# HGRN heads as a pipeline of levels and states, with the first pair's queries and forget gates made by seven products and kept in DRAM

## The chip, the cores and the metric

The kernel runs on one core of one Trainium2 chip. A core has TensorE (PE in the profile, its weight loads PEld), VectorE (DVE), ScalarE (ACT), GpSimd (POOL) and SyncE (SP), which issues most of the DMA. The metric is the device time of one execution in microseconds, as the median of several runs. Every engine works through its own row of instructions in the order in which the program puts them; a scheduler in the building layer sets that order, so it is not the order of the Python lines.

## The reference

One layer of a decoder trunk over 1024 tokens of width 1024, all in float32. A combined projection `u @ w_in` gives ten groups of columns, and two branches mix the tokens. What the change touches is the first branch, HGRN2, with 8 heads of 128:

```python
q = silu(q)                                   # per head (S, 128)
f = lb + (1 - lb) * sigmoid(zf);  k = (1 - lb) * sigmoid(-zf)
S_t = diag(f_t) S_{t-1} + k_t^T v_t           # state 128 x 128
o_t = S_t^T q_t                               # then head norm and output gate
```

The second branch is retention with 4 heads. Both are projected (`w_pa`, `w_pb`), merged by gates, projected again (`w_o`) and normed; then comes an MLP with a squared ReLU.

## The kernel before

Each float32 product is made of three products of rounded parts (`mm3`, lines 182 to 186: high by high, high by low, low by high), 128x128 weights against 512 columns. A plain tile of 128 output columns takes 8 blocks of rows, so 24 such products for each half of the tokens (`dense_T`, line 383). Where four blocks are needed together, `seven` (line 437) makes 2x2 blocks with seven products instead of eight: 84 large products for a group of 256 columns instead of 96. A `use_...` function then takes each of the group's four result blocks.

The program runs in stages.

- A start stage makes the scaled input and four gate tiles.
- A first stage by sevens makes the row-wise groups `hi`, `rv`, `rg` (`seven_rows`) and then 16 kept groups (`hg`, `ga`, `rq`, `rk`; list `kept`, lines 1563 to 1574), whose results go to DRAM by DMAs that GpSimd issues.
- A second stage has plain products. `r_head(0)`, the first retention head, is woven with the last eight halves of the gate `gb` (`gate_proj`). Then come the HGRN heads.
- After them the first part of retention's merge (`r_first`: 16 pieces of 12 products with `w_pb`), the other retention heads with the HGRN merge (`r_fill`), the output projection and the MLP.

An HGRN head has two parts, both in `h_rec` (line 796). In the levels the scores of 128 tokens are built from 2 tokens upward: VectorE scales q and k by products of forget gates (lines 804 to 868), TensorE multiplies k by the scaled q (lines 811 and 847, into two PSUM banks of the kind `a`), and VectorE copies the wanted entries into the score tile with masks (lines 814, 815, 862). In the states TensorE transposes k (line 878) and then, for each of eight chunks, adds state and score parts of the output (889, 890) and makes the update (895), which VectorE adds to the state (898, 900). Norm, transposes (920) and the gate (924) follow some steps later through a list of deferred calls (`later`, `tick`).

`h_rec` gives way 9 times in the levels and 10 times in the states, and one head follows the other. Between its steps `h_fill` puts halves of the plain projections `hq` and `hf` (`h_cols`, line 765): four halves of 24 products a head. Six halves of the first pair go ahead of all, then 26 are woven with 123 steps; the last 31 steps are mixed with 14 pieces of `r_first` and five steps of retention head 1. The scaled q of a head lives in one large tile `hX` from its first level to its last chunk.

Large tiles come from 14 buffers (`U`), the gates f and k from 4 buffers (`fk`). Retention head 0 uses the same `fk` buffers and six of the `U` buffers for its own states.

Of the kernel before, what the change touches and what calls it, by code (L numbers as in the profile page):

```python
# [19 lines left out]
P = 128  # L20
# [3 lines left out]
HH = 8  # L24
# [29 lines left out]
PB_END, R1_N, R1_AT = 36, 5, 20  # L54
# [3 lines left out]
H_DEFER = (6, 8)  # L58
# [72 lines left out]
class Trunk:  # L131
# [590 lines left out]

    def use_turned(self, dst):
# [29 lines left out]
    def h_dense(self, p):  # L753
        self.hst[p] = [dict(), dict()]
        self.h_values(p)
        for hd in (0, 1):
            for what in ("hq", "hf"):
                yield from self.h_cols(p, what, hd)

    def h_fill(self, begun):  # L760
        yield from begun
        for p in range(1, 4):
            yield from self.h_dense(p)
# [26 lines left out]
    def h_values(self, p):  # L790
        v = self.hv[p % 2]
        self.hst[p][0]["v"] = self.hst[p][1]["v"] = v
# [3 lines left out]
    def h_rec(self, p, hd):  # L796
# [3 lines left out]
        q, f, k, v = s["q"], s["f"], s["k"], s["v"]  # L800
# [27 lines left out]
        for ln, sz in enumerate(H_SIZES):  # L828
# [5 lines left out]
            D4 = self.xp.tile([P, B], F32, tag=f"D{2 * ln + 2}", bufs=1, name=self.uid("D"))  # L834
# [32 lines left out]
            V.tensor_tensor(Xv[:, 0, 1], Xv[:, 0, 1], by(Dv[:, 0], B, sz), op=ALU.mult)  # L867
            V.tensor_tensor(Xv[:, 0, 2:4], Xv[:, :, 2], by(D2v[:, 0], 2, B, sz), op=ALU.mult)
            Dt = D4
        yield  # L870
        state = None
        for hf in (0, 1):
# [7 lines left out]
            nc.scalar.activation(kt, pb, AF.Copy)  # L880
            ob, sq = (self.e2().rearrange("p (c e) -> p c e", c=4) for _ in (0, 1))
            ms = self.xp.tile([P, 4], F32, tag="ms", bufs=2, name=self.uid("ms"))
            for c in range(4):
                n = 4 * hf + c
                cs = slice(n * P, n * P + P)
                vn = v[:, n, hd * P:(hd + 1) * P]
                po = self.ps("c", (P, P))
                if n > 0:
                    nc.tensor.matmul(po, qp[:, cs], state, start=True, stop=False)
# [3 lines left out]
                if n < 7:  # L893
# [7 lines left out]
                    state = ns  # L901
                yield
            nc.vector.tensor_scalar(ms, ms, 1.0 / P, HEAD_EPS, op0=ALU.mult, op1=ALU.add)
            rs = self.xp.tile([P, 4], F32, tag="rs", bufs=2, name=self.uid("rs"))
            nc.gpsimd.tensor_tensor(rs, ms, self.mhalf[:, :4], op=ALU.pow)
            self.later(2, lambda ob=ob, rs=rs, hf=hf, g=g: self.h_scale(p, h, hf, ob, rs, g))
            yield

    def h_scale(self, p, h, hf, ob, rs, g):
# [4 lines left out]
        self.later(H_DEFER[p // 3] - 2, lambda: self.h_out(h, hf, ob, g))  # L914
# [12 lines left out]
    def h_pair_rec(self, p, heads=(0, 1)):  # L927
        for hd in heads:
            for _ in self.h_rec(p, hd):
                self.tick()  # L930
                yield
        while heads[-1] == 1 and p == 3 and self.pend:
            self.tick()
            yield

# [603 lines left out]
def build(ctx, tc, ins, out):  # L1539
# [11 lines left out]
    k.or_d = dt("or_d", RH, 512)  # L1551
    k.rq_d, k.rk_d = dt("rq_d", RH, 256), dt("rk_d", RH, 256)
# [16 lines left out]
    for h in range(RH):  # L1569
# [3 lines left out]
        kept.append((("rk", h), C_RK + 256 * h, k.use_turned(k.rk_d[h])))  # L1573
    kept += light
# [3 lines left out]
    for p in range(4):  # L1578
# [67 lines left out]
    with ExitStack() as s:  # L1646
# [3 lines left out]
        weave(k.gate_proj("gb", k.gb_d, range(4, KT)), k.r_head(0), 8, 12)  # L1650
# [9 lines left out]
        begun = k.h_dense(0)  # L1660
        for _ in range(6):
            k.tick()
            next(begun)
        rec = (x for p in range(4) for x in k.h_pair_rec(p))
        weave(k.h_fill(begun), islice(rec, 123), 26, 123)
        pb, r1 = k.r_first(), k.r_head(1)
        for _ in range(2):
            next(pb)
        mix((rec, 31, 0, 31), (pb, 14, 0, PB_END), (r1, R1_N, R1_AT, 36))
# [81 lines left out]
```

## Time and profile before

| what | value |
|---|---|
| median of the runs shown | 2287.32 us (2284.84 to 2288.99) |
| the profiled execution's own time | 2287.82 us |
| its span, first to last instruction | 2286.0 us |
| mean granted clock of TensorE | 0.997 |
| kept groups by sevens | about 490 to 766 us |
| retention head 0 with gates | about 766 to 868 us |
| first product of an HGRN head (line 804) | 879.4 us for the first head, 1151.2 us for the eighth |

A stretch is named by its times from the span's start. In a row of busy time by stretch each engine has its busy microseconds and, in brackets, its instructions; then come the granted clock, the busy share of the DMA engines and what they moved in GB/s. In a row of the groups by line stand busy time and mean ns of one instruction, and behind the next bar the engine's idle time just before them. A row of the waits names who waited, for whom, the sum, how often, and the longest. TensorE's float32 matmuls leave two records each, its transposes and rounded products one. Matmuls overlap, so two that follow each other at full speed start closer together than their listed length.

### The profile page before, as it was taken

How to read it: one execution, taken by the hardware profiler on the slowest of the kernel's cores; microseconds unless marked ns; L12 is line 12 of the kernel's file. 1: busy time of each engine (PE TensorE's matmuls, PEld its weight loads, DVE VectorE, ACT ScalarE, POOL GpSimd, SP SyncE). 2: the span in 40 equal slices, each digit the busy share in tenths (PEclk: the TensorE clock that was granted, in tenths of full speed). 3: DMA queues.
4: the chain of work that ended last, by engine and by line, in shares of the span. 5: the costliest groups of instructions: out<-in, count | busy, mean ns of one | idle time of the engine just before them, and what ended most of it. 6: DMA issues, size and time to landing. Idle time of an engine off the chain costs nothing.

```text
span 2286.0 us, 29888 instructions
## 1 busy us (share of the span) xinstructions
PE 2239.7 (98%) x10366; PEld 1847.6 (81%) x10366; DVE 1642.2 (72%) x3054; ACT 1013.8 (44%) x1861; POOL 290.8 (13%) x458
## 2 busy tenths in 40 slices
PE   7999999999999999999999999999999999999998
PEld 5888888888888788888877788888878888888886
DVE  8966768686778465788866667767896666668778
ACT  4433434453333362333446556222475555643441
POOL 0111011111111020010011222013112111100001
PEclk9999999999999999999999999999999999999999
DMA  9766655533333542121225666864244444877863
GB/s 277 239 216 230 228 187 198 173 120 111 111 111 102 176 152 83 42 88 56 88 92 178 232 197 213 298 211 164 84 159 173 152 152 152 280 263 239 260 219 116
DMA packets 227320, 389.85 MB, mean 171 GB/s; under 512 B 17480, under 2 KB 122688, under 8 KB 226400
## 3 DMA queue, kind: packets, MB, share of 16 engines
q1 hardware_dynamic: 197376, 291.20, 39.5%
q0 software_dynamic: 29616, 96.67, 11.4%
q8 instruction: 82, 1.34, 0.2%
q14 instruction: 70, 0.57, 0.1%
q10 hardware_dynamic: 176, 0.06, 0.0%
HBM read 286.14 MB, written 101.72 MB: 170 GB/s over the span
## 4 chain that ended last, share of the span: by engine, by line
PE 69%; issue 17%; DVE 5%; DMA 4%; POOL 3%; ACT 2%; SPq 0%; POOLq 0%; DVEq 0%; ACTq 0%
PE psd L185 13%; PE psd L186 13%; PE psd L184 13%; PE psa L185 3%; PE psa L184 3%; PE psa L186 3%; PE psc L185 3%; PE psc L184 3%; PE psc L186 3%; PE psb L1130 2%; PE psa L847 2%; PE psb L185 1%; PE psb L186 1%; PE psb L184 1%; PE psc L1116 1%
## 5 line engine op out<-in xcount | busy, mean ns | idle before, releaser
L184 PE MATMUL psd<-U,wh 128*128 128x512 f32 x760 | 305.7, 404 | 3.5 <-ACT e L1224 2.2
L185 PE MATMUL psd<-U,wh 128*128 128x512 f32 x760 | 303.4, 399 | 2.8 <-DVE U L180 2.8
L186 PE MATMUL psd<-U,wl 128*128 128x512 f32 x760 | 302.0, 398 | 0.0
L179 ACT ACTIVATE bh<-s 128x512 fp32r<-128x512 f32 x204 | 128.0, 633 | 247.6 <-PE psd L185 62.0
L184 PE MATMUL psd<-U,bh 128*128 128x512 f32 x496 | 193.0, 389 | 1.8 <-DVE e L446 1.8
L179 ACT ACTIVATE bh<-raw 128x512 fp32r<-128x512 f32 x153 | 97.2, 637 | 217.2 <-PE psd L185 85.8
L185 PE MATMUL psd<-U,bh 128*128 128x512 f32 x496 | 193.1, 389 | 0.1
L186 PE MATMUL psd<-U,bl 128*128 128x512 f32 x496 | 193.0, 389 | 0.0
L180 DVE TENSOR_TENSOR bl<-raw,bh 128x512 fp32r<-128x512 f32 x153 | 104.5, 689 | 113.0 <-ACT bh L179 112.6
L180 DVE TENSOR_TENSOR bl<-s,bh 128x512 fp32r<-128x512 f32 x204 | 139.2, 687 | 61.6 <-ACT bh L179 61.4
L184 PEld LDWEIGHTS psd<-U,wh 128*128 128x128 f32 x760 | 142.9, 189 | 32.6 <-ACT U L179 3.6
L185 PEld LDWEIGHTS psd<-U,wh 128*128 128x128 f32 x760 | 143.9, 189 | 30.9 <-DVE U L180 5.1
L186 PEld LDWEIGHTS psd<-U,wl 128*128 128x128 f32 x760 | 143.7, 189 | 27.5
L179 ACT ACTIVATE wh<-raw 128x512 fp32r<-128x512 f32 (+1 forms) x87 | 61.3, 729 | 207.0 <-PE psd L185 187.7
L179 ACT ACTIVATE U<-hr 128x512 fp32r<-128x512 f32 x112 | 70.4, 630 | 145.8 <-issue 80.2
L180 DVE TENSOR_TENSOR U<-hr,U 128x512 fp32r<-128x512 f32 x112 | 77.0, 687 | 51.4 <-ACT U L179 51.3
L184 PEld LDWEIGHTS psd<-U,bh 128*128 128x128 f32 x496 | 93.1, 188 | 21.7 <-DVE e L446 2.6
L185 PEld LDWEIGHTS psd<-U,bh 128*128 128x128 f32 x496 | 93.1, 188 | 19.8 <-DVE U L180 0.5
L186 PEld LDWEIGHTS psd<-U,bl 128*128 128x128 f32 x496 | 93.1, 188 | 19.4
L184 PE MATMUL psa<-U,bh 128*128 128x512 f32 x248 | 96.7, 390 | 1.9 <-ACT e L434 1.9
L180 DVE TENSOR_TENSOR wl<-raw,wh 128x512 fp32r<-128x512 f32 (+1 forms) x87 | 69.9, 817 | 37.6 <-ACT wh L179 35.1
L185 PE MATMUL psa<-U,bh 128*128 128x512 f32 x248 | 96.5, 389 | 0.0
(431 smaller groups left out, 5577.8 us busy)
## 6 DMA issues: line engine op xcount, KB each, us to landing
raw<-in_w_in SPq DMA_DIRECT2D x146, 512.0 KB
raw<-in_w_down SPq DMA_DIRECT2D x64, 512.0 KB
raw<-in_w_ada SPq DMA_DIRECT2D x32, 512.0 KB
raw<-in_w_up SPq DMA_DIRECT2D x32, 512.0 KB
raw<-in_w_pb SPq DMA_DIRECT2D x20, 512.0 KB
adw<-in_w_ada SPq DMA_DIRECT2D x16, 512.0 KB
v_d<-e POOLq DMA_DIRECT2D x32, 256.0 KB, 4.3
rg_d<-e POOLq DMA_DIRECT2D x32, 256.0 KB, 2.6
```

The source lines that it names most:

```text
L179: self.nc.scalar.activation(hi, src, AF.Copy)
L180: self.nc.vector.tensor_tensor(lo, src, hi.bitcast(F32), op=ALU.subtract)
L184: r = mm(out, wh, uh, start=start, stop=False, skip_group_check=more)
L185: mm(out, wh, ul, start=False, stop=False, skip_group_check=more)
L186: return r, mm(out, wl, uh, start=False, stop=stop, skip_group_check=more)
L847: nc.tensor.matmul(pa[:, c * 192:(c + 1) * 192].rearrange("p (b w r) -> p b w r", w=2, r=3 * sz), k[:, n * P:(n + 1) * P], mv, start=True, ...
L1116: mm(G[e], l[:, n % 2, es], r, start=n == 0 and i == 0, stop=i == 2, skip_group_check=n > 0)
L1130: mm(po, l, r, start=i == 0, stop=i == len(pairs) - 1)
```

## The change

It does three things.

- The groups `hq` and `hf` of the first pair of heads become two more kept groups of the first stage. `use_query` and `use_forget` make q, f and the sigmoid for k there, and GpSimd's DMAs store them to `q_d`, `f_d`, `k_d`. In the second stage `h_load` brings them back, and `h_fill` covers only pairs 1 to 3.
- `h_rec` is split into `h_levels` and `h_states`. `h_stream` takes one step of the states of head h-1 and one of the levels of head h in turn, nine of each, so that 81 steps hold all heads. The last level writes the scaled q into two small tiles `Q` (with two copies on ScalarE), so that `hX` is free for the next head, and the last scan factors get two buffers.
- The weaving has new numbers. One half of the gate `gb` comes ahead of retention head 0, five are woven with it, two come behind. Of the 81 steps, 4 to 63 are mixed with 24 halves, from 63 on with the 16 pieces of `r_first`, and from 72 on with three steps of retention head 1.

```diff
+H_SEVEN = (0,)
+GB_N, H_LOAD = 5, 5
+H_FILL = 63
+PB_END, R1_N, R1_AT = 85, 3, 72
-H_DEFER = (6, 8)
+H_DEFER = ((1, 2), (2, 3))
+H_STEPS = 9
...
+    def use_query(self, p):
+        def use(m, half, src, bank):
+            ...
+            nc.scalar.activation(sg, src, AF.Sigmoid)
+            nc.vector.scalar_tensor_tensor(tv, pr, self.omlb[:, h:h + 1], sr, op0=ALU.mult, op1=ALU.mult)
+            nc.gpsimd.dma_start(self.q_d[h].rearrange("p (w b) -> p w b", w=2)[:, :, half * 256:half * 256 + 256], tv)
+    def use_forget(self, p):
+        def use(m, half, src, bank):
+            ...
+            nc.scalar.activation(f, src, AF.Sigmoid)
+            nc.scalar.activation(t, src, AF.Sigmoid, scale=-1.0)
+            nc.scalar.activation(f, f, AF.Identity, scale=self.omlb[:, h:h + 1], bias=self.lb[:, h:h + 1])
+            nc.gpsimd.dma_start(self.f_d[h][:, sl], f)
+            nc.gpsimd.dma_start(self.k_d[h][:, sl], t)
...
+    def h_load(self, p, hd):
+        s["q"], s["f"], s["k"] = self.hq[hd], self.e4(), self.e4()
+        nc.sync.dma_start(s["q"][:, 0:2], self.q_d[h].rearrange("p (w b) -> p w b", w=2))
+        nc.sync.dma_start(s["f"], self.f_d[h])
+        nc.sync.dma_start(s["k"], self.k_d[h])
...
+            if last:
+                Q = s["Q"] = [self.e2() for _ in (0, 1)]
+                for hf in (0, 1):
+                    nc.scalar.activation(Qv[:, 0], Xv[:, 0, 0, bs], AF.Copy)
+                    V.tensor_tensor(Qv[:, 1], Xv[:, 0, 1, bs], by(Dv[:, 0, bs], B // 2, sz), op=ALU.mult)
+                    V.tensor_tensor(Qv[:, 2:4], Xv[:, :, 2, bs], D2v[:, 0, bs].unsqueeze(1).to_broadcast([P, 2, B // 2]).unsqueeze(3).to_broadcast([P, 2, B // 2, sz]), op=ALU.mult)
...
-                    nc.tensor.matmul(po, qp[:, cs], state, start=True, stop=False)
+                    nc.tensor.matmul(po, Q[hf][:, c * P:(c + 1) * P], state, start=True, stop=False)
...
+    def h_stream(self):
+        states = iter(())
+        for h in range(HH + 1):
+            p, hd = divmod(h, 2)
+            levels = self.h_levels(p, hd) if h < HH else iter(())
+            if hd == 1 and p < 3:
+                self.h_values(p + 1)
+            for n in range(H_STEPS):
+                next(states, None)
+                next(levels, None)
+                ...
+                self.tick()
+                yield
+            if h < HH:
+                states = self.h_states(p, hd)
...
+    for p in H_SEVEN:
+        kept += [(("hq", p), C_HQ + 256 * p, k.use_query(p)), (("hf", p), C_HF + 256 * p, k.use_forget(p))]
...
-        weave(k.gate_proj("gb", k.gb_d, range(4, KT)), k.r_head(0), 8, 12)
+        gates = k.gate_proj("gb", k.gb_d, range(4, KT))
+        drain(islice(gates, 1))
+        weave(islice(gates, GB_N), k.r_head(0), GB_N, 12)
...
-        begun = k.h_dense(0)
-        for _ in range(6):
-            k.tick()
-            next(begun)
-        weave(k.h_fill(begun), islice(rec, 123), 26, 123)
-        mix((rec, 31, 0, 31), (pb, 14, 0, PB_END), (r1, R1_N, R1_AT, 36))
+        for hd in (0, 1):
+            k.h_load(0, hd)
+            if hd == 0:
+                k.h_values(0)
+        rec, pb, r1 = k.h_stream(), k.r_first(), k.r_head(1)
+        mix((gates, 6 - GB_N, 0, 4), (rec, 4, 0, 4))
+        nf, n = 8 * (4 - len(H_SEVEN)), 9 * H_STEPS
+        mix((rec, n - 4, 4, n), (k.h_fill(), nf, 4, H_FILL), (pb, 16, H_FILL, PB_END), (r1, R1_N, R1_AT, n))
```

What this does to the engines' rows is seen at three places. Line numbers of the changed kernel are 4 higher up to `h_cols`, some 40 higher in the levels (804 became 844, 811 became 851, 847 became 888) and 58 to 78 higher behind (878 became 936, 889 to 895 became 953 to 959, 920 became 986, 1103 became 1181).

On SyncE, before, at the end of retention head 0: its last loads of `rg_d` and `v_d`, the values of the first pair (`hi_d`), and then weights.

```order
L1103 DMA e_7449<-rg_d_93 128x512
L1084 DMA e_7452<-v_d_89 128x512
L794 DMA U_7558<-hi_d_97 128x8x256
L1103 DMA e_7522<-rg_d_93 128x512
L336 DMA raw_7169<-in_w_in 128x4x256
```

On SyncE now, at the same place: the loads of q, f and k of both heads of the pair stand there.

```order
L1162 DMA e_7768<-v_d_89 128x512
L800 DMA hq_7844<-q_d_103 128x1024
L801 DMA fk_7848<-f_d_111 128x1024
L1181 DMA e_7810<-rg_d_93 128x512
L802 DMA fk_7849<-k_d_119 128x1024
L834 DMA U_7846<-hi_d_97 128x8x256
L800 DMA hq_7845<-q_d_104 128x1024
L801 DMA fk_7854<-f_d_112 128x1024
L802 DMA fk_7855<-k_d_120 128x1024
```

The six loads are in front of the weights, and the last load of retention head 0 (`rg_d`) stands between them. On VectorE, before, where retention head 0 ends: its last norm (lines 1154 to 1157), then the q of the dense halves (786), weight splits (180), and only then the first head's product of q and f (804).

```order
L1154 BN_AGGR stat_7535<-stat_7535 128x2
L1155 TENSOR_SCALAR stat_7535<-stat_7535 128x1
L1157 SCALAR_TENSOR_TENSOR U_7066<-U_7066,stat_7535,e_7522 128x512
L786 SCALAR_TENSOR_TENSOR hq_7556<-psd_7575,small,e_7600 128x2x256
L180 TENSOR_TENSOR wl_7640<-raw_7165,wh_7639 128x512
L786 SCALAR_TENSOR_TENSOR hq_7556<-psd_7611,small,e_7636 128x2x256
L180 TENSOR_TENSOR wl_7640<-raw_7167,wh_7639 128x512
L180 TENSOR_TENSOR wl_7712<-raw_7169,wh_7711 128x512
L804 TENSOR_TENSOR hq_7556<-hq_7556,fk_7645 128x512
```

On VectorE now, at the same place (844 is the product of q and f, 1231 to 1235 retention head 0's last norm, 865, 880 and 881 the scan factors):

```order
L844 TENSOR_TENSOR hq_7844<-hq_7844,fk_7848 128x512
L865 TENSOR_TENSOR hq_7844<-fk_7848 128x512
L1231 BN_STATS stat_7823<-U_7416 128x6
L880 TENSOR_TENSOR D_7961<-hq_7844 128x2x128
L1232 BN_AGGR stat_7823<-stat_7823 128x2
L881 TENSOR_TENSOR D_7962<-D_7961 128x128
L1233 TENSOR_SCALAR stat_7823<-stat_7823 128x1
L1235 SCALAR_TENSOR_TENSOR U_7416<-U_7416,stat_7823,e_7810 128x512
```

The product that needs the loaded q and f has moved ahead of retention head 0's last norm. On TensorE, before, in the first head's states (psc): transposes of k (878), then chunk by chunk the products 889, 890 and 895, with large products (184 to 186) between.

```order
L895 MATMUL psc_7979<-U_7558,e_7970 128x128
L878 MATMUL psb_8050<-cst,fk_7646 128x128 x4
L186 MATMUL psd_8143<-U_272,wl_7774 128x512
L184 MATMUL psd_8143<-U_272,wh_7773 128x512
L889 MATMUL psc_8018<-st_7981,U_7555 128x128
L890 MATMUL psc_8018<-U_7558,U_7550 128x128
L895 MATMUL psc_8023<-U_7558,e_7970 128x128
```

On TensorE now, in the states of the fourth head: the first bank products (851) of the next head's levels stand between the chunks (953, 954, 959).

```order
L954 MATMUL psc_9291<-U_7847,U_7838 128x128
L959 MATMUL psc_9295<-U_7847,e_9257 128x128
L851 MATMUL psa_9299<-hq_7844,fk_8965 128x3x64 x2
L851 MATMUL psa_9304<-hq_7844,fk_8965 128x3x64 x2
L986 MATMUL psb_9309<-cst,e_9090 128x128 x4
L953 MATMUL psc_9317<-st_9297,e_9238 128x128
L954 MATMUL psc_9317<-U_7847,U_7838 128x128
L959 MATMUL psc_9322<-U_7847,e_9257 128x128
L188 MATMUL psd_9383<-U_296,wh_8958 128x512
L189 MATMUL psd_9383<-U_297,wh_8958 128x512
L851 MATMUL psa_9326<-hq_7844,fk_8965 128x3x64 x2
```

Levels of one head and states of the one before it share TensorE's row. All large products together are 8412 in the row before and 8388 now.

More of the change, by code (lines that the diff above doesn't have):

```diff
@@ L721, in use_gate @@
         return use
+    def use_query(self, p):
+        def use(m, half, src, bank):
+            nc = self.nc
+            h = 2 * p + m
+            sg, t = self.et(), self.et()
+            nc.scalar.activation(sg, src, AF.Sigmoid)
+            pr, sr = (a.rearrange("p (b two) -> p two b", two=2) for a in (src, sg))
+            tv = t.rearrange("p (two b) -> p two b", two=2)
+            nc.vector.scalar_tensor_tensor(tv, pr, self.omlb[:, h:h + 1], sr, op0=ALU.mult, op1=ALU.mult)
+            nc.gpsimd.dma_start(self.q_d[h].rearrange("p (w b) -> p w b", w=2)[:, :, half * 256:half * 256 + 256], tv)
+        return use
+    def use_forget(self, p):
+        def use(m, half, src, bank):
+            nc = self.nc
+            h = 2 * p + m
+            sl = slice(half * 512, half * 512 + 512)
+            f, t = self.et(), self.et()
+            nc.scalar.activation(f, src, AF.Sigmoid)
[3 more added lines that the diff above has]
+            nc.gpsimd.dma_start(self.k_d[h][:, sl], t)
+        return use
     def use_turned(self, dst):
@@ L758, in h_dense, with h_fill @@
                 yield from self.h_cols(p, what, hd)
[L760 to L763, printed above, removed]
+    def h_fill(self):
+        for p in range(4):
+            if p not in H_SEVEN:
+                yield from self.h_dense(p)
+    def h_load(self, p, hd):
+        nc = self.nc
+        h = 2 * p + hd
+        s = self.hst.setdefault(p, [dict(), dict()])[hd]
+        s["q"], s["f"], s["k"] = self.hq[hd], self.e4(), self.e4()
+        nc.sync.dma_start(s["q"][:, 0:2], self.q_d[h].rearrange("p (w b) -> p w b", w=2))
+        nc.sync.dma_start(s["f"], self.f_d[h])
+        nc.sync.dma_start(s["k"], self.k_d[h])
     def h_cols(self, p, what, hd):
@@ L880, in h_rec @@
             nc.scalar.activation(kt, pb, AF.Copy)
+            return g, kt
+        state = None
+        nxt = turned(0)
+        yield
+        for hf in (0, 1):
+            g, kt = nxt
             ob, sq = (self.e2().rearrange("p (c e) -> p c e", c=4) for _ in (0, 1))
@@ L925, in h_out @@
         nc.gpsimd.dma_start(self.oh_d[h][:, hf * 512:hf * 512 + 512], ot)
-    def h_pair_rec(self, p, heads=(0, 1)):
-        for hd in heads:
-            for _ in self.h_rec(p, hd):
+    def h_stream(self):
[8 more added lines that the diff above has]
+                next(levels, None)
+                if n == H_LOAD and h > 0 and (h + 1) // 2 in H_SEVEN:
+                    self.h_load((h + 1) // 2, (h + 1) % 2)
                 self.tick()
                 yield
-        while heads[-1] == 1 and p == 3 and self.pend:
+            assert next(levels, None) is None
+            if h < HH:
+                states = self.h_states(p, hd)
+        while self.pend:
             self.tick()
@@ L1577, in build @@
     plain = [k.spec_T(w_in, 0, C_GB + 256 * m, ("gb", m), ("U" if m == 2 else "w", "w")) for m in (2, 3)]
-    for p in range(4):
+    for p in (p for p in range(4) if p not in H_SEVEN):
         plain.append(k.in_turn(*(k.spec_T(w_in, 0, c0 + 256 * p, (c, p)) for c, c0 in (("hq", C_HQ), ("hf", C_HF)))))
```

53 lines of the change are left out of this document (30 added, 23 removed).

## The prediction

> **What bounds the kernel now.** I read the page's busy times first, then busy time by stretch of the span, then the waits inside those stretches.
>
> ```profile
> span 2286.0 us, 29888 instructions
> PE 2239.7 (98%) x10366; PEld 1847.6 (81%) x10366; DVE 1642.2 (72%) x3054; ACT 1013.8 (44%) x1861; POOL 290.8 (13%) x458
> ...
> PE 69%; issue 17%; DVE 5%; DMA 4%; POOL 3%; ACT 2%; SPq 0%; POOLq 0%; DVEq 0%; ACTq 0%
> ```
>
> TensorE is busy 98% of the span, and the chain that ended last is its own work. Matmuls overlap, so busy time hides small losses; the price of a product is its spacing. The stretches below are: sixteen groups by seven products; retention head 0 with gate products; the first dense halves and the first HGRN head; four whole HGRN heads; the last two heads; the join to the last retention heads; these heads; and ten microseconds inside the last-two-heads stretch.
>
> ```profile
> core 0: us, PE busy (x) PEld busy (x) DVE busy (x) ACT busy (x) POOL busy (x), PEclk, DMA share, GB/s
> 490.00:766.00 276.00, 275.72 (x1217) 228.07 (x1216) 198.45 (x319) 104.70 (x175) 31.34 (x59) 1.00 0.34 113
> 766.00:868.00 102.00, 99.72 (x475) 81.22 (x474) 48.58 (x85) 50.28 (x86) 19.82 (x31) 1.00 0.48 160
> 868.00:949.80 81.80, 81.15 (x409) 68.24 (x408) 54.48 (x137) 26.43 (x66) 3.15 (x4) 1.00 0.22 71
> 949.80:1113.50 163.70, 161.84 (x883) 137.67 (x881) 132.90 (x357) 59.99 (x183) 12.83 (x16) 1.00 0.19 63
> 1113.50:1235.00 121.50, 114.76 (x620) 96.11 (x619) 83.74 (x207) 55.57 (x172) 15.47 (x23) 0.99 0.31 107
> 1235.00:1290.00 55.00, 51.15 (x237) 39.31 (x236) 42.60 (x71) 38.03 (x61) 14.18 (x21) 1.00 0.75 255
> 1223.00:1233.00 10.00, 10.00 (x62) 8.93 (x61) 4.41 (x10) 5.99 (x21) 1.17 (x3) 0.83 0.27 93
> ```
>
> The first row gives the price: 276.00 us for 1217 products of 512 columns, 0.227 us each, with nothing lost. TensorE's visible idle time lies elsewhere: 2.3 us with retention head 0, 6.7 us in the last two HGRN heads (121.50 less 114.76), 3.9 us at the join. In the last two heads the granted clock also falls to 0.83 over ten microseconds, worth 1.7 us more. Four heads in the middle take 163.70 us, 40.9 each, and VectorE is busy 132.90 of them: 33.2 a head, 81%. So TensorE bounds every stage, with VectorE closest behind it in the HGRN heads.
>
> What a head costs TensorE comes from these rows of the groups by line and of the chain; the times at the chain's front are for so many matmuls in a row.
>
> ```profile
> L847 PE MATMUL psa<-U,fk 128*128 128x192 f32 x384 | 73.4, 330 | 1.7 <-DVE U L862 0.7 <-ACT U L855 0.4 <-DVE U L837 0.4
> L811 PE MATMUL psa<-hq,fk 128*128 128x192 f32 x128 | 26.5, 329 | 0.2 <-ACT U L855 0.2
> L889 PE MATMUL psc<-st,U 128*128 128x128 f32 x112 | 24.9, 304 | 4.1 <-ACT e L891 2.6 <-ACT e L892 0.8 <-DVE st L900 0.4
> L890 PE MATMUL psc<-U,U 128*128 128x128 f32 x128 | 24.7, 275 | 0.0
> L895 PE MATMUL psc<-U,e 128*128 128x128 f32 x112 | 22.5, 283 | 1.6 <-ACT e L891 0.8 <-ACT e L880 0.7
> L920 PE MATMUL psb<-cst,e 128*128 128x128 f32 x64 | 9.7, 273 | 0.0
> L878 PE MATMUL psb<-cst,fk 128*128 128x128 f32 x64 | 9.6, 273 | 0.0
> ...
> 916.18 1.30 PE psa L847 x8
> 1301.11 1.78 PE psa L1064 x16
> ```
>
> Levels: 64 records a head at 1.30/8 = 0.1625 us, 10.4 us. States: 60 records a head at 1.78/16 = 0.111 us, 6.7 us. Together 17.1 us. The four dense halves a head (24 products each) are 21.8 us. Sum 38.9, measured 40.9: 2.0 us a head are lost to small waits and to changing between small and large matmuls.
>
> **The change, part by part.** All of it is set against the profiled execution: 2287.8 us, of which the span is 2286.0; the median of the shown runs, 2287.3, lies 0.5 us lower.
>
> *Products.* The four column tiles of pair 0 took 8 halves of 24 products; by sevens, two groups take 7 blocks of 12 each: 168 instead of 192. 24 x 0.227 = **-5.4 us**, with bounds close by, since both stages run at that spacing. The 12 stores that it adds go through GpSimd's queue, 13% busy. In the stage that takes the two groups, VectorE is busy 198.45 of 276.00 and ScalarE 104.70: the added sigmoids and products find room there, and TensorE idles 0.28 us in it now. I cost them at nothing; were ScalarE to hold up a weight split, it would be one or two split lengths, a microsecond.
>
> *Start of retention head 0.*
>
> ```profile
> PE psa L1050 <- DMA e<-rq_d: 1.8, 1, 1.8
> ...
> 782.10 6.41 DMA e<-v_d
> 788.57 5.67 DMA e<-rq_d
> ```
>
> TensorE waits 1.8 us for the retention loads. Now a whole gate half is issued ahead, and the order puts eight more large products (1.8 us) before the first transposes that need them: **-1.8 us** (bounds -1.8 and 0).
>
> *Rest of retention head 0.* Five gate halves are woven in instead of eight; three have gone ahead of it or behind it. From about its fourth block on, the blocks follow each other with hardly a large product between.
>
> ```profile
> 817.49 2.06 PE psb L1130 x9
> ...
> 821.59 2.05 PE psb L1130 x9
> ```
>
> Two such blocks stand 4.10 us apart now; their 15 products and four transposes are 3.85 us. So about 0.25 us is lost per bare block, 1 us over four: **+1 us** (0 to 2).
>
> *Start of the HGRN heads.* Before, six dense halves (32.7 us) stood between retention head 0 and the first bank of levels. Now the head's q, f and k come from DRAM and about 15 us of TensorE work (50 large products, 11.4; 17 transposes, 1.9; two banks, 1.3) lie between the retention product that frees the buffers of f and k and the second pair of banks. VectorE must in that time get the loads, make q*f and its scan factors, finish retention's last norm and copy two banks. Its rows:
>
> ```profile
> L814 DVE COPY_PREDICATED U<-mask,psa 128x256 f32<-128x256 uint8 x32 | 14.1, 452 | 7.1 <-PE psa L811 7.0
> L815 DVE COPY_PREDICATED U<-mask,psa 128x128 f32<-128x128 uint8 x32 | 14.0, 443 | 0.4
> L820 DVE TENSOR_TENSOR U<-hq,fk 128x1024 f32<-128x1024 f32 x8 | 9.8, 1224 | 1.3 <-PE psc L889 1.3
> L837 DVE TENSOR_TENSOR U<-U,hq 128x512 f32<-128x512 f32 x8 | 5.5, 693 | 0.2
> ```
>
> Four copies (1.8), L820's product (1.2), four of the 512-wide kind (2.8) and the small ones, some 3, make 9 us behind a landing; with the 5.67 us of the 256 KB load in the chain above that is 14.7, about even with the cover. The second head's q and f, for which VectorE stops a little later in its row, stand behind 3.4 MB of loads. At the 255 GB/s of the join they land after 13 us, at the 160 GB/s of retention head 0 after 21. I take **+2.5 us**, nearer to the fast row, since nothing else loads there; bounds 0 and +8 (21 less 15, and the copies behind). The Trainium skill (DMA: Bandwidth & Descriptors, Anatomy of one DMA) fits a transfer, measured on the GpSimd path, as 2.0 us plus bytes over 436 GB/s. By that estimate the loads land after 9.8 us and this term would be 0, the sum 2.5 us lower; the 256 KB loads above (5.67 us in the chain) are slower than its 2.6.
>
> *The heads in the middle.* While dense halves last, 59 steps (6.6 heads) carry 24 of them: 3.66 a head, 20.0 us, and 17.1 of its own: 37.1. With today's loss of 2.0 a head it would be 39.1; the shorter head is work already counted, not gain. But the margin of VectorE shrinks (33.2 of 39.1 is 85%), and in its row state updates of one head now stand between copies of the next.
>
> ```profile
> DVE U L862 <- PE psa L847: 11.2, 16, 1.1
> DVE st L900 <- PE psc L895: 7.2, 10, 1.1
> DVE st L898 <- PE psc L895: 3.8, 4, 1.0
> DVE U L814 <- PE psa L811: 3.0, 10, 0.3
> ```
>
> These are its waits for TensorE in the four-head stretch: 25.2 us, 6.3 a head. 33.2 + 6.3 = 39.5: its own loop is as long as TensorE's. Where two loops are that even, each adds some of the other's waits: I take 0.5 us a head, **+3.3 us**; bounds 0, and +11.9 (the head stays at 40.9, 1.8 more than 39.1).
>
> *The last two heads.* Their 6.7 us of idle time and the 1.7 us of clock come from one head's states standing alone, with too few products of w_pb between (14 pieces over the end). The longest single wait there is short:
>
> ```profile
> PE psd L184 <- ACT e L1224: 1.7, 1, 1.7
> PE psc L889 <- ACT e L891: 1.4, 2, 0.7
> ```
>
> The Trainium skill (TensorE: Matmul & The Clock Gate, Part 1) has the clock halve after an idle window of about 3.4 us. Here it halved for that long (0.83 over 10 us) with no listed wait over 1.7, so the row decides: many short waits are enough. By that rule a start of the heads at its bound of 8 us idle would halve the clock too and cost 1.7 us more, 2288.6 in all.
>
> Now head 6's states lie under head 7's levels, 16 w_pb pieces of 2.7 us begin when the dense halves end, and only head 7's nine state steps are bare, each with a piece beside it. I leave 2.4 of the 8.4 us: **-6 us** (bounds -8.4 and -2). The join stays as it was, since the last output must still go to DRAM and back.
>
> Sum: -5.4 - 1.8 + 1 + 2.5 + 3.3 - 6 = -6.4; 2287.8 - 6.4 = 2281.4, and about 2281 against the median.
>
> **The rivals.** *VectorE becomes the bound (slower).* If every one of a head's seven state updates makes VectorE wait as L900 does now (7.2/10 = 0.72 us), that is 5.0 instead of 1.8 a head, its loop is 42.7, and 6.6 x (42.7 - 39.6) = 20 us come on top: 2302. For it: 85%, and a queue with two heads' work in one row. Against it: the order puts levels between the products on which a state update waits. It decides from 40.6 us a head on; there the gain of 6.4 is gone. Chance 0.13.
>
> *Late loads (no change).* The loads land at the slow rate, VectorE stands at q*f with retention's last norm behind it, and TensorE waits the 8 us of the upper bound: 2287. For it: no dense half is left as cover. Against it: the queue has little else. Chance 0.11.
>
> *The waits only move (no change).* The last heads keep their idle time, for instance because head 7's states now meet all that was put at the end: -0.4 us, 2287. Chance 0.13.
>
> *More than forecast.* The start costs nothing, the middle nothing more than today, the end its whole 8.4 and half of the 3.9 us at the join: -5.4 - 1.8 - 8.4 - 2 = -17.6, 2270. For it: the pipeline gives TensorE two independent heads to take work from. Against it: VectorE's 85%. Chance 0.11.
>
> **How the numbers follow.** The forecast has the other 0.52; its own range is 2275 to 2287. The range from 2270 to 2291 takes in all but the VectorE rival and the outermost starts. 0.2% is 4.6 us, about what a measurement of this kernel tells from no change. Faster: 0.9 of the forecast and the large gain, 0.58. Same: the rest of the forecast, the moved waits and most of the late loads, 0.27. Slower: the VectorE rival, and the worst of the late loads, 0.15.
>
> **What would show it.** In the profile after: 24 fewer large products; no wait of TensorE for rq_d; starts of successive heads 39 to 40.5 us apart while dense halves last (over 40.6: VectorE rival, with its busy share near 85% and longer waits for L959); a wait of 1 to 4 us of TensorE for VectorE at the first head (8: late loads); under 3 us idle in the last two heads and no dip of the clock. If the product count falls by 24 and the time doesn't fall, the middle terms were mis-sized.

## The result, and the profile after

| | before | after |
|---|---|---|
| median | 2288.15 us (2284.84 to 2289.6, 4 runs) | 2265.87 us (2264.62 to 2269.01, 4 runs) |
| ratio, 95% interval | | 0.9907 (0.989 to 0.9924) |
| profiled span | 2286.0 us | 2264.0 us |
| a second set, timed with the last experiments | 2287.99 us | 2270.38 us, 0.992 (0.9906 to 0.9933) |

The change saves 18 to 22 us where 6.4 were forecast. The direction was right. The first median lies outside the stated range of 2270 to 2291, the second at its edge. These lines of the page of the changed kernel answer to the first ones of before: span, busy times and instructions, and the engines' shares of the chain that ended last.

```profile
span 2264.0 us, 29935 instructions
PE 2224.8 (98%) x10342; PEld 1847.5 (82%) x10342; DVE 1649.2 (73%) x3090; ACT 1026.4 (45%) x1889; POOL 299.6 (13%) x470
...
PE 91%; DVE 2%; DMA 2%; issue 2%; ACT 1%; POOL 1%; SPq 0%; DVEq 0%; ACTq 0%; POOLq 0%
```

TensorE has 24 matmuls fewer (10366 before), and still 98% of the span. Busy time by stretch, in the order of the stretches shown of before: groups by seven products; retention head 0 and the start of the heads; five heads in the middle; the last two heads in two pieces; what follows them.

```profile
core 0: us, PE busy (x) PEld busy (x) DVE busy (x) ACT busy (x) POOL busy (x), PEclk, DMA share, GB/s
528.00:804.00 276.00, 276.00 (x1220) 228.52 (x1219) 195.11 (x308) 105.17 (x179) 34.27 (x63) 1.00 0.34 116
804.00:900.00 96.00, 93.91 (x450) 76.07 (x449) 55.53 (x104) 49.50 (x85) 21.07 (x32) 1.00 0.59 204
930.60:1117.60 187.00, 186.87 (x1053) 165.52 (x1051) 157.25 (x448) 75.13 (x233) 17.87 (x20) 1.00 0.19 65
1105.00:1181.00 76.00, 75.05 (x424) 65.79 (x423) 65.20 (x171) 39.53 (x124) 10.75 (x15) 1.00 0.34 116
1181.00:1223.00 42.00, 38.69 (x217) 32.47 (x216) 18.33 (x31) 26.90 (x72) 8.73 (x14) 1.00 0.47 164
1223.00:1275.00 52.00, 51.64 (x236) 41.93 (x236) 38.41 (x68) 32.25 (x51) 11.58 (x17) 0.97 0.79 262
```

The stage by seven products runs at the price of before (276.00 over 1220 products). The third row is the surprise: five heads (930.6 and 1117.6 are starts of line 863, the same place in two heads) take 187.0 us, 37.4 each, where the forecast said 39.6. TensorE is busy 186.87 of 187.00, and VectorE, 84% busy, holds nothing up. TensorE's waits at the start of the heads (the first line), and then in the last two heads:

```profile
PE psa L1243 <- ACT U L1236: 1.6, 2, 1.4
...
PE psb L986 <- ACT e L977: 3.3, 1, 3.3
PE psa L888 <- ACT U L896: 0.6, 1, 0.6
```

No wait for `rq_d` is left. One long wait stands at the very end, where the last head's output is scaled (977) before it is turned (986).

**Lost time.** Small losses don't show in busy time, so I took from each trace, for every matmul, the time until the next one starts, less the median of that time for the same shape in the same trace. The sum over the medians is called work, the sum of the differences lost time. The stretches are: to the first transposes of retention head 0; to the first bank of levels; 240 us from there on, some six heads; from there to the last head's last output; all that follows.

| us | work | to retention 0 | to first bank | heads, 240 us | heads, rest | after | lost in all |
|---|---|---|---|---|---|---|---|
| before | 2209.4 | 22.5 | 1.2 | 10.9 | 14.6 | 15.3 | 64.5 |
| after | 2203.6 | 22.1 | 3.9 | 4.7 | 7.5 | 9.9 | 48.2 |
| after, second execution | 2203.4 | 21.0 | 4.0 | 4.6 | 7.3 | 17.1 | 54.0 |

Work fell by 5.8 us. Lost time fell by 16.3 in one execution and by 10.5 in another; in both, the heads give 13 of it, and the stretch after them is what differs.

### The profile page after: what moved, and what is told of

Same layout as the page of the kernel before. It is cut to its first block, busy times and chain, and to the rows that moved or that the text cites. A ratio compares the mean times of both kernels' runs of the same rounds, so it can differ in the third digit from the quotient of the medians.

```text
span 2264.0 us, 29935 instructions
## 1 busy us (share of the span) xinstructions
PE 2224.8 (98%) x10342; PEld 1847.5 (82%) x10342; DVE 1649.2 (73%) x3090; ACT 1026.4 (45%) x1889; POOL 299.6 (13%) x470
## 3 DMA queue, kind: packets, MB, share of 16 engines
q0 software_dynamic: 30576, 99.82, 11.9%
## 4 chain that ended last, share of the span: by engine, by line
PE 91%; DVE 2%; DMA 2%; issue 2%; ACT 1%; POOL 1%; SPq 0%; DVEq 0%; ACTq 0%; POOLq 0%
PE psd L189 17%; PE psd L190 17%; PE psd L188 17%; PE psa L189 5%; PE psa L188 5%; PE psa L190 5%; PE psc L189 3%; PE psc L188 3%; PE psc L190 3%; PE psa L888 2%; PE psb L1208 2%; PE psb L190 1%; PE psb L189 1%; PE psb L188 1%; PE psc L1194 1%
## 5 line engine op out<-in xcount | busy, mean ns | idle before, releaser
L188 PE MATMUL psd<-U,wh 128*128 128x512 f32 x696 | 279.6, 404 | 0.0
L189 PE MATMUL psd<-U,wh 128*128 128x512 f32 x696 | 277.0, 398 | 1.8 <-DVE U L184 1.8
L190 PE MATMUL psd<-U,wl 128*128 128x512 f32 x696 | 276.6, 398 | 0.0
L188 PE MATMUL psd<-U,bh 128*128 128x512 f32 x528 | 205.5, 389 | 1.3 <-DVE e L450 1.3
L189 PE MATMUL psd<-U,bh 128*128 128x512 f32 x528 | 205.5, 389 | 0.0
L190 PE MATMUL psd<-U,bl 128*128 128x512 f32 x528 | 205.4, 389 | 0.0
L189 PEld LDWEIGHTS psd<-U,wh 128*128 128x128 f32 x696 | 131.5, 189 | 27.0 <-DVE U L184 3.4
L190 PEld LDWEIGHTS psd<-U,wl 128*128 128x128 f32 x696 | 131.4, 189 | 25.4
L188 PEld LDWEIGHTS psd<-U,wh 128*128 128x128 f32 x696 | 130.8, 189 | 24.6 <-ACT U L183 1.0
L188 PEld LDWEIGHTS psd<-U,bh 128*128 128x128 f32 x528 | 99.1, 188 | 22.5 <-DVE e L450 2.1
L189 PEld LDWEIGHTS psd<-U,bh 128*128 128x128 f32 x528 | 99.1, 188 | 21.2 <-DVE U L184 0.5
L190 PEld LDWEIGHTS psd<-U,bl 128*128 128x128 f32 x528 | 99.1, 188 | 20.5
L188 PE MATMUL psa<-U,bh 128*128 128x512 f32 x264 | 102.9, 390 | 0.4 <-ACT e L438 0.3
L189 PE MATMUL psa<-U,bh 128*128 128x512 f32 x264 | 102.7, 389 | 0.0
L190 PE MATMUL psa<-U,bl 128*128 128x512 f32 x264 | 102.7, 389 | 0.0
```

Source lines behind the costliest of these rows:

```text
L188: r = mm(out, wh, uh, start=start, stop=False, skip_group_check=more)
L189: mm(out, wh, ul, start=False, stop=False, skip_group_check=more)
L190: return r, mm(out, wl, uh, start=False, stop=stop, skip_group_check=more)
```

## The experiments

The theory after the result: what came beyond the products comes from the pipeline, because a state step that stands alone makes TensorE wait, and under another head's levels it doesn't. The rivals: it comes from pair 0's way (no dense halves before the first head, gate halves moved, less work on ScalarE and VectorE), or from the last two heads alone. Beside that stood the question why VectorE had not become the bound. Diffs are against the changed kernel. The lost time of all of them but 5 and 6 is in one table behind the first four.

**1. The pipeline alone** (label pipe_only): pair 0 by dense halves again, in the places of before.

```
-H_SEVEN = (0,)
+H_SEVEN = ()
...
+        weave(k.gate_proj("gb", k.gb_d, range(4, KT)), k.r_head(0), 8, 12)
...
+        begun = k.h_dense(0)
+        for _ in range(6):
+            k.tick()
+            next(begun)
...
+        mix((rec, n, 0, n), (k.h_fill(begun), 26, 0, H_FILL), (pb, 16, H_FILL, PB_END), (r1, R1_N, R1_AT, n))
```

> The pipeline over heads alone: pair 0's queries and forget gates are dense halves again, six of them ahead of the first head as in the kernel before, all eight gate halves are woven with retention head 0, and nothing goes through DRAM for them. Theory (the pipeline saves what came beyond the products): the 5.4 us of products and the 1.8 us of the rq_d wait are not gained, nearly all of the rest is, so 2271 to 2275 us; in the profile the loss of TensorE in the heads falls as in the changed kernel (from about 19 us to about 8). Rival (the gain beyond the products comes from pair 0's way: no dense halves before the first head, three gate halves moved, less work on VectorE and ScalarE per head): 2284 to 2290. By the prediction's own terms for the middle and the last heads (+3.3 and -6) it would be 2285.

Measured: 2274.83 us, ratio 0.9941 (0.9928 to 0.9953): 15 us of the change's 18 to 22. The theory had it. The lost time in the heads is halved, 12.7 us against 25.5 in the table below, where the expectation named about 8 and 19.

**2. Pair 0 by seven products alone** (label seven_only): levels and then states of one head, twice nine steps.

```
-H_DEFER = ((1, 2), (2, 3))
+H_DEFER = ((2, 4), (2, 6))
...
+            for part in (self.h_levels(p, hd), self.h_states(p, hd)):
+                for n in range(H_STEPS):
+                    next(part, None)
+                    self.tick()
+                    yield
...
+        nf, n = 8 * (4 - len(H_SEVEN)), 16 * H_STEPS
+        mix((rec, n - 4, 4, n), (k.h_fill(), nf, 4, 116), (pb, 16, 116, 150), (r1, R1_N, 128, n))
```

> Pair 0 by seven products and through DRAM alone, with the gate halves where the change puts them: the states of a head follow its own levels again, a step at a time, and the dense halves and w_pb pieces are spread over the steps in the proportion of the kernel before. The copy of the scaled queries at the last level stays. Theory (pipeline): only products, the rq_d wait and a start that costs some 2 us are left, so -5.4 - 1.8 + 2 = -5, 2283 us; the heads in the middle stay about 2 us above their work. Rival (pair 0's way): 2266 to 2272.

Measured: 2280.17 us, 0.9966 (0.9952 to 0.9979), 9 us faster than before against 5 expected, and 10 to 14 us slower than with the pipeline. The two parts alone make 24 us, the whole 18 to 22: they add up, near enough.

**3. The overlap at the last two heads alone** (label last_two).

```
-H_DEFER = ((1, 2), (2, 3))
+H_DEFER = ((2, 4), (2, 3))
...
+            if h < 7:
+                for _ in range(H_STEPS if h > 0 else 0):
+                    next(states, None)
+                    self.tick()
+                    yield
             for n in range(H_STEPS):
                 next(states, None)
                 next(levels, None)
...
+        nf, n = 8 * (4 - len(H_SEVEN)), 15 * H_STEPS
+        mix((rec, n - 4, 4, n), (k.h_fill(), nf, 4, 117), (pb, 16, 117, 139), (r1, R1_N, 126, n))
```

> The changed kernel with the states of heads 0 to 5 after the head's own levels, as in the kernel before, and only head 6's states under head 7's levels; dense halves and w_pb pieces in the same proportion to the heads. It splits the pipeline's gain between the middle and the last two heads. The prediction's terms say that the overlap costs 3.3 us in the middle and saves 6 at the end: this kernel would then be faster than the changed one, 2262 to 2265. Theory now (the overlap saves in the middle too, about 1 us a head, since the loss of 2.0 us a head came from the states standing alone): the serial sevens kernel had 2280, the end gives back 5 to 7 of it, so 2273 to 2275, some 8 above the changed kernel. Rival (all of the gain lies in the last two heads): 2266.

Measured: 2282.6 us, 0.9976 (0.9967 to 0.9986). A miss: the overlap at the end alone gains nothing against the serial order. The prediction's terms would have made this the fastest of all.

**4. The overlap everywhere but there** (label first_six): head 6's states alone, then head 7's levels.

```
+            if h == 7:
+                for _ in range(H_STEPS):
+                    next(states, None)
+                    self.tick()
+                    yield
...
+        nf, n = 8 * (4 - len(H_SEVEN)), 10 * H_STEPS
+        mix((rec, n - 4, 4, n), (k.h_fill(), nf, 4, 66), (pb, 16, 66, 92), (r1, R1_N, 81, n))
```

> The complement of the run with the overlap at the last two heads alone: here heads 0 to 6 are pipelined, and head 6's states stand alone before head 7's levels. With the overlap at the end alone nothing was gained against the serial order (2282.6 against 2280.2, each against the kernel before: 0.9976 and 0.9966). If the gain is the middle's (about 0.6 us a head less lost by TensorE, since no product waits for a state alone, 7 us in all), this kernel keeps 7 of the 14 us or more: 2271 to 2274. If the overlap pays only as a whole, because each waits for the other, it stays near 2280.

Measured: 2267.9 us, 0.9913 (0.9899 to 0.9927): as fast as the changed kernel, and 3 us faster than the theory named. The overlap of heads 0 to 6 carries the pipeline's whole gain, as far as the spread between executions lets it be told.

The same 187 us of the span, 930 to 1117, in six traces; all of it lies in the heads. TensorE's busy time is the first number behind the length, VectorE's the third. Before, then seven_only, then last_two:

```profile
930.00:1117.00 187.00, 184.49 (x1003) 157.01 (x1002) 151.86 (x404) 69.58 (x212) 15.02 (x20) 1.00 0.19 63
```

```profile
930.00:1117.00 187.00, 182.47 (x1005) 157.28 (x1004) 153.12 (x428) 70.35 (x218) 15.86 (x20) 1.00 0.19 64
```

```profile
930.00:1117.00 187.00, 182.98 (x1003) 156.16 (x1002) 151.17 (x419) 70.56 (x221) 16.25 (x20) 1.00 0.19 64
```

The pipelined ones, pipe_only, first_six and the changed kernel's second execution:

```profile
930.00:1117.00 187.00, 186.82 (x1052) 165.36 (x1052) 159.08 (x451) 75.96 (x237) 16.52 (x19) 1.00 0.19 64
```

```profile
930.00:1117.00 187.00, 186.77 (x1059) 165.27 (x1058) 161.28 (x458) 75.50 (x236) 18.00 (x21) 1.00 0.20 65
```

```profile
930.00:1117.00 187.00, 186.89 (x1051) 165.50 (x1050) 157.33 (x447) 74.52 (x231) 16.96 (x20) 1.00 0.19 65
```

Two groups with nothing between: some 1004 matmuls and 2.5 to 4.5 us of TensorE idle with states in series, some 1054 and 0.2 us with states under levels. VectorE is busier in the second group (157 to 161 us against 151 to 153) and yet delays nobody.

| us | work | to retention 0 | to first bank | heads, 240 us | heads, rest | after | lost in all |
|---|---|---|---|---|---|---|---|
| pipe_only | 2209.4 | 23.3 | 1.3 | 5.0 | 7.7 | 15.5 | 52.7 |
| seven_only | 2203.5 | 20.0 | 2.9 | 11.9 | 11.7 | 15.6 | 62.1 |
| last_two | 2203.3 | 21.3 | 3.0 | 12.2 | 12.9 | 17.6 | 67.1 |
| first_six | 2201.9 | 20.1 | 3.7 | 6.0 | 8.0 | 14.9 | 52.6 |
| dve_more | 2203.1 | 19.1 | 3.9 | 4.3 | 15.0 | 14.4 | 56.7 |
| dve_most | 2203.2 | 22.4 | 5.6 | 7.1 | 18.0 | 13.2 | 66.3 |
| flush | 2203.5 | 19.3 | 3.7 | 4.6 | 4.7 | 19.0 | 51.2 |
| flush_more | 2203.6 | 21.6 | 3.8 | 4.7 | 11.3 | 13.0 | 54.4 |

The column of the first 240 us sorts the kernels: 10.9 to 12.2 in series, 4.6 to 6.0 with the pipeline, whatever is done with pair 0 (4.3 and 7.1 with more work for VectorE, experiments 7 and 8). The start (to the first bank) costs 1.7 to 2.8 us more with pair 0 from DRAM, and 4.4 in dve_most.

The traces also show where in these 240 us TensorE lost the time. Directly ahead of the products of the states (889, 890 and 895 before) it lost 7.3 us before, 8.4 in seven_only and 7.5 in last_two, but 2.3 in the changed kernel, 2.2 in pipe_only and 2.8 in first_six. Ahead of the levels' products the same kernels lost 2.2 to 3.4, in no order. One more rival is out by the same traces, that the new weaving changes less often between small and large matmuls: there are 146 such changes before, 158 in seven_only and 165 in last_two, and 149, 134 and 150 in the changed kernel, pipe_only and first_six.

**5. VectorE's own loop** (label two_pairs): two pairs by seven products, so that two and a half heads have no large product beside them.

```
-H_SEVEN = (0,)
+H_SEVEN = (0, 1)
...
+        mix((rec, n - 4, 4, n), (k.h_fill(), nf, 27, H_FILL), (pb, 16, H_FILL, PB_END), (r1, R1_N, R1_AT, n))
```

> Pairs 0 and 1 by seven products and through DRAM, dense halves only for pairs 2 and 3, from step 27 on: steps 4 to 27, two and a half heads, have no large product beside the levels and states, so that VectorE's own loop can be read there as the distance of the heads. By the prediction (33.2 us busy and 6.3 us of waits that belong to the loop) the bare heads stand 39.5 us apart, TensorE idles 2.5 x 22 = 57 us and the sum is 2266 - 5.5 + 57 = 2317. If the waits were VectorE waiting for a TensorE that was itself the bound, so that they vanish when TensorE has nothing else, the heads stand 32 to 34 us apart, TensorE idles about 40 us: 2300.

**6. The same in the serial order** (label two_serial): experiment 2 with two pairs, dense halves from step 54 of 144.

```
-H_SEVEN = (0,)
+H_SEVEN = (0, 1)
...
+        nf, n = 8 * (4 - len(H_SEVEN)), 16 * H_STEPS
+        mix((rec, n - 4, 4, n), (k.h_fill(), nf, 54, 117), (pb, 16, 116, 150), (r1, R1_N, 128, n))
```

> Pairs 0 and 1 by seven products and through DRAM as in the run with two pairs, but with the states after the head's own levels; heads 1 and 2 have no large product beside them. There VectorE's loop can be read in the serial order. With the pipeline these heads stood 33.2 us apart. If the 39.5 us of the prediction (33.2 busy, 6.3 waiting) were the loop of the serial order, the heads stand 39 to 41 us apart here, and the pipeline is what took the waits out of VectorE's loop. If the serial loop is 33 to 34 as well, the waits were never part of VectorE's loop. Time: 2300 + 9 of the pipeline's other gain + 0 or 2.5 x 6.5, so 2309 or 2325.

Measured: 2299.87 us, 1.0046 (1.0026 to 1.0066), and 2317.23 us, 1.0129 (1.0111 to 1.0148): the first at its lower forecast, the second between its two. Two bare heads, from the start of line 863 in one to the same line two heads on, first pipelined (967.1, 1000.0, 1034.1):

```profile
967.10:1034.10 67.00, 46.87 (x248) 42.56 (x249) 57.14 (x169) 20.11 (x75) 8.96 (x8) 0.85 0.20 71
```

Then in series (966.6, 1004.6, 1042.5):

```profile
966.60:1042.50 75.90, 51.68 (x253) 42.92 (x252) 58.72 (x170) 20.09 (x75) 6.66 (x8) 0.78 0.19 63
```

The bare head takes 33.5 us pipelined and 38.0 in series. VectorE's work is the same (57.14 and 58.72), its idle time is not: 4.9 us a head against 8.6. So such waits are no fixed part of VectorE's loop: they change with the order of the program. That 38.0 lies near the prediction's 39.5 proves little, because a bare head has less work for VectorE (28.6 and 29.4 us, against 33.2 with dense halves between). Nor is all of the 4.5 us shown to be the order's: the granted clock was lower in series (0.78 against 0.85), and TensorE was busy 2.4 us a head longer there. VectorE's waits for TensorE in these two windows, pipelined and then in series:

```profile
DVE U L903 <- PE psa L888: 6.8, 15, 1.1
...
DVE st L964 <- PE psc L959: 0.3, 1, 0.3
```

```profile
DVE U L903 <- PE psa L888: 11.6, 15, 1.7
DVE st L964 <- PE psc L959: 1.6, 2, 0.8
```

**7 and 8. More work for VectorE** (labels dve_more, and dve_most with 5 in place of 3).

```
-        V.tensor_tensor(q[:, 2], q[:, 1], fv[:, 1], op=ALU.mult)
+        for _ in range(3):
+            V.tensor_tensor(q[:, 2], q[:, 1], fv[:, 1], op=ALU.mult)
...
+        for _ in range(3):
+            V.tensor_tensor(qp.rearrange("p (b two) -> p two b", two=2), q[:, 0::2],
+                            fv[:, 0].unsqueeze(1).to_broadcast([P, 2, T // 2]), op=ALU.mult)
```

> The changed kernel with two products of VectorE made three times in each head (q times f of 512 columns, and the 1024-wide product of queries and f): the same values are written again, 2 x (0.69 + 1.22) = 3.8 us more a head on VectorE, on the way from one level to the next. By the prediction, VectorE's loop was as long as TensorE's (39.5 against 39.6), so every microsecond counts: 6.6 heads x 3.8 = 25 us, 2291. If VectorE has the margin that its busy share leaves (31.5 of 37.5 us), 31.5 + 3.8 = 35.3 still fits: 2266 to 2271.

> The changed kernel with the two products of VectorE made five times in each head instead of three times: 4 x (0.69 + 1.22) = 7.7 us more a head than the changed kernel. With three times it cost 12 us by the medians. VectorE's own loop, read at the heads without large products, was 33.2 us; 33.2 + 7.7 = 40.9 is over TensorE's 37.5 by 3.4, so if VectorE then sets the pitch of seven heads, 7 x 3.4 = 24 us and more: 2290 to 2295. By the prediction's loop of 39.5 each microsecond counts from the first: 8 x 7.7 = 61, 2327. If the cost only grows in proportion to the first dose: 2290.

Measured: 2278.18 us, 0.9953 (0.9938 to 0.9969), 8 to 12 above the changed kernel's two medians; and 2287.55 us, 0.9999 (0.999 to 1.0008), 17 to 22 above. The first lies between its forecasts of 2266 to 2271 and 2291, the second 2 us under the lowest of its own. Five heads in the middle, with 3.8 us more a head:

```profile
929.70:1116.00 186.30, 186.30 (x1051) 165.29 (x1050) 172.50 (x468) 74.37 (x231) 18.13 (x20) 1.00 0.19 66
```

And with 7.7 us more, with VectorE's longest waits there:

```profile
937.30:1137.20 199.90, 197.51 (x1096) 172.54 (x1095) 191.84 (x495) 80.81 (x240) 23.04 (x20) 1.00 0.20 67
```

```profile
DVE U L905 <- PE psa L890: 3.1, 11, 0.6
DVE ms L971 <- ACT e L958: 1.1, 3, 0.7
```

With the first dose VectorE is 93% busy and the heads are as near to each other as without it (186.30 us for five, 187.00 without it). In the trace the cost falls wholly on the last heads, where no dense halves lie between: 15.0 us lost there against 7.5, most of it in one wait for ScalarE's copies of a level of the last pair:

```profile
PE psa L890 <- ACT U L898: 6.3, 2, 4.8
```

With the second dose VectorE is 96% busy, the head takes 40.0 us (199.90/5), and VectorE's idle time has shrunk to 1.6 us a head. So the waits of 6 us a head that it shows in the unloaded kernels are slack: they go as soon as it has more to do. The 40.0 isn't the price of the dose, though. TensorE has 45 more matmuls in these five heads than with the first dose, 37 of them large products, and idles 2.4 us. Here, too, most of what is lost beyond the changed kernel falls on the last heads: 18.0 us against 7.5.

**9 and 10. The last outputs** (labels flush, flush_more): the steps reach five further, so that the last scaling lies between w_pb pieces; in the second also two more pieces of retention head 1 there, and the turn a step later.

```
-        mix((rec, n - 4, 4, n), ...
+        mix((rec, n + 1, 4, n + 5), ...
```

```
+H_DEFER = ((1, 2), (2, 4))
...
+        mix((rec, n + 1, 4, n + 5), (k.h_fill(), nf, 4, H_FILL), (pb, 16, H_FILL, PB_END), (r1, 5, R1_AT, n + 5))
```

> The changed kernel with its steps spread five further, so that the last two outputs of the last head are scaled and turned between the last w_pb pieces and not all at once behind them. In the changed kernel TensorE waits 3.3 us there for ScalarE's scaling (L986 for L977). Theory: that wait goes and 2 to 3 us are saved, 2263. Rival: ScalarE is behind for the splits of the next weights, and the wait moves to the next products: 2266.

> The changed kernel with its steps spread five further as in the run before, two more pieces of retention head 1 among them, and the last head's outputs turned one step later. Spreading alone took the 3.3 us wait away and gave it back in retention head 1 (2.0 us at L1208 and 1.0 at a product) and at the last join. Theory: with more of retention's pieces between, the wait doesn't come back there, 2262 to 2264. Rival: what is won at the end is lost at the next wait for ScalarE or VectorE, 2266 to 2269.

Measured: 2269.07 us, 0.9917 (0.9903 to 0.9931), and 2271.57 us, 0.9928 (0.9915 to 0.9942); no gain, as the rivals said, and some 3 us above their figures. TensorE's waits in flush, from the last states on:

```profile
PE psb L1208 <- DVE e L990: 1.8, 1, 1.8
PE psd L189 <- DVE U L184: 0.8, 1, 0.8
...
PE psb L986 <- ACT e L977: 0.2, 1, 0.2
```

The wait of 3.3 us is down to 0.2, and 2.6 us of it stand at the next two places, behind VectorE, where the rival had named ScalarE. This trace also holds the wait of experiment 11 (3.0 us). Against the changed kernel's second execution, which has that wait too, its lost time is 2.8 us less, so a small gain isn't ruled out. With more pieces between, in flush_more, one wait of 5.0 us for a weight split stands in their place:

```profile
PE psa L1142 <- DVE U L184: 5.0, 1, 5.0
```

**11. The changed kernel once more** (label after_again, no edit).

> The changed kernel once more, unaltered, for the spread between executions: 2264 to 2268. Its first trace has a wait of 1.0 us for ScalarE at the join of the last retention head (L1243 for L1236) with no dip of the clock behind it; other runs of this study show 3.0 to 3.3 us there and some ten products at half the clock behind it, about 4 us together. If that is chance from execution to execution, this trace or its times may show either; if it belongs to the order, the wait is 1.0 again.

Measured: 2270.38 us (2267.32 to 2271.38), 0.992 (0.9906 to 0.9933), above the range expected. At the join of the last retention head the first execution lost 1.3 us, this one 5.1: the wait, and the ten microseconds around it.

```profile
PE psa L1243 <- ACT U L1236: 3.1, 1, 3.1
```

```profile
1418.00:1428.00 10.00, 9.49 (x37) 7.72 (x38) 5.63 (x11) 1.05 (x2) 0.79 (x1) 0.83 1.01 409
```

In the first execution of the changed kernel the same place, with a wait of 1.0 us ahead of it:

```profile
1417.00:1427.00 10.00, 10.00 (x46) 8.27 (x45) 5.79 (x12) 0.04 (x1) 0.79 (x1) 1.00 1.01 412
```

So this wait differs from execution to execution of one program. The two profiled executions are 5.6 us apart. 3.8 us of it lie here, and 2.2 at a wait ahead of line 1128: 1.3 us for ScalarE in the first execution, 2.0 us for the load of `rk_d` in the second, with the clock down behind it. What makes these waits long or short wasn't found.

## Why the prediction was wrong, step by step

| us | forecast | first trace | second trace |
|---|---|---|---|
| products | -5.4 | -5.8 | -6.0 |
| first stage, beside the products | 0 | +1.7 | +0.5 |
| wait for rq_d | -1.8 | -2.1 | -2.0 |
| rest of retention head 0 and start of the heads | +3.5 | +2.7 | +2.8 |
| heads in the middle | +3.3 | -6.2 | -6.3 |
| last two heads | -6 | -7.1 | -7.3 |
| after the heads | 0 | -5.4 | +1.8 |
| sum | -6.4 | -22.2 | -16.5 |

The measured columns are differences of the table of lost time (the first stretch split at the end of the groups by seven) and of the work. They make the spans' differences, -22.0 and -16.4.

*Products, the wait for rq_d, retention head 0 and start.* Right, within a microsecond each. At the start VectorE did wait for the loads (3.4 us for `f_d` in two waits), and TensorE's one longer wait there was 1.4 us, behind retention head 0's last norm on ScalarE.

*Heads in the middle.* This is the step that failed: "33.2 + 6.3 = 39.5: its own loop is as long as TensorE's." The 6.3 us are waits of VectorE for TensorE, in a stage where TensorE was the bound; they were added to VectorE's work as if it could not do without them. Such a sum comes out near the distance of the heads whatever the loop is: 33.2 busy and all of VectorE's 7.7 us of idle time a head are the 40.9. Experiment 7 gave VectorE 3.8 us more a head and the heads stayed at 37.3 us; experiment 8 brought its idle time down to 1.6 us. In the bare heads, too, the idle time goes with the order, 4.9 us a head in the pipeline and 8.6 in series. The second half of the error is in "with today's loss of 2.0 a head": that loss was put down to small waits and to changing between small and large matmuls and was carried over. Most of it came from the states in series: ahead of their products TensorE lost 7.3 of 240 us before and 2.3 after, with as many changes between small and large matmuls (146 and 149). With the pipeline five heads take 37.4 each against 37.1 of work by the prediction's own sum. The forecast thus asked what the new order would cost the engine that was not the bound, and not what it would spare the one that was.

*Last two heads.* The size was about right (-7 against -6), the reason was not. Head 6's states under head 7's levels were to bring it; that alone brought nothing (last_two loses 12.9 us in the rest of the heads, seven_only 11.7), and without it the gain was there (first_six, 8.0). Nor did the idle time fall under 3 us (0.95 and 3.31 in the two pieces), nor did the dip of the clock go: it stands behind the 3.3 us wait now. What in the order of the earlier heads makes the last ones lose less was not told apart.

*After the heads.* "The join stays as it was" was wrong as well. TensorE's idle time at the join fell from 3.9 us (1235 to 1290 in the prediction's table) to 0.4 (1223 to 1275 after). By the lost time, the first 100 us behind the last head's last output cost 8.5 us before, and 4.3 and 4.1 in the two executions after. Part of that only moved ahead of the output: in flush, where the 3.3 us wait for line 977 is gone, the same 100 us cost 7.0. Further on the two executions differ by the waits of experiment 11 (5.6 and 13.0 us, 6.8 before); the trace of before has no wait at the place of the longer one.

*The rivals.* VectorE as the bound, late loads and waits that only move are out. "More than forecast" (2270) had the size, but by luck: it let the middle cost nothing and the start vanish, where the middle gave 6 us and the start cost about what was forecast. Its part for the join was right in kind (-2 there, some -4 measured). The prediction's range was too narrow on that side because the loss of 2.0 us a head was in no case allowed to go.

## What to carry to other kernels

The waits of an engine for the one that bounds the stage can be slack, as they were here, and don't simply add to its own loop; to know the loop, take the bound engine's other work away or load the engine until something gives. When two serial chains are interleaved, ask first how much of the bound engine's present loss stems from one of them standing alone. And a long wait can differ between two executions of one program, so a difference of 4 us between two traces needs a second trace.

## What the runs showed of the hardware

The length of a single wait of TensorE didn't tell whether the granted clock fell behind it. Behind the 3.3 us wait for line 977 in the changed kernel it was 0.83 over ten microseconds:

```profile
1218.00:1228.00 10.00, 6.71 (x34) 5.77 (x33) 6.71 (x8) 8.06 (x15) 1.68 (x3) 0.83 0.57 185
```

In the second execution it was 0.83 behind the 3.1 us of experiment 11 and also behind the 2.0 us for `rk_d` (1350 to 1360 us). But it stayed at 1.00 behind 3.7 us in dve_more (1222 to 1232 us, the wait for the same scaling) and behind 3.1 us in dve_most (890 to 900 us). It also stayed at 1.00 behind the waits of 1.0 to 1.4 us in the changed kernel's first trace. Where it fell, 0.83 over ten microseconds is worth some 1.7 us. The Trainium skill (TensorE: Matmul & The Clock Gate, Part 1) halves the clock after an idle window of about 3.4 us. With single waits taken for that window, the dip behind 2.0 us and the full clock behind 3.7 don't agree with it, nor does the dip of the kernel before, with no listed wait over 1.7. What decides wasn't found. In the bare heads of experiments 5 and 6 the mean clock was 0.85 and 0.78, with TensorE busy 70% and 68% of the time.
